# Where the pieces of a side matrix are loaded from: GpSimd's queue or the weights' queue

## The chip, the cores and the metric

One Trainium2 chip; the program runs on one NeuronCore. The metric is the device time of one execution in microseconds. Three executions of the kernel before took 2799.04, 2801.40 and 2794.86 us; the median is 2799.04 us.

## What is computed

Two transformer blocks, one after the other, on 256 tokens of width 2048, in float32. The second block also sees 256 context tokens (`ctx`). Both streams of the second block are normalised and then shifted and scaled by vectors that come out of one big matrix:

```python
def adaln(cond, w_ada, b_ada):
    return jnp.split(jax.nn.silu(cond) @ w_ada + b_ada, ADA_CHUNKS, axis=-1)
...
m_lat = [m[:, None, :] for m in adaln(c, w_ada[l], b_ada[l])]
m_ctx = adaln(c_ctx, w_ada[l], b_ada[l])
hc = modulate(rms_norm_2(ctx, norm1_g[l]), m_ctx[0], m_ctx[1])
h = modulate(rms_norm_2(x, norm1_g[l]), m_lat[0], m_lat[1])
```

`w_ada` is 2048 x 12288 in float32, 100.7 MB, and is multiplied by one vector (two for the first third). It depends on nothing that the first block computes, so the kernel works on it beside the other matrices, long before it is needed.

## The kernel before, in words

**The weights.** All other matrices are cut into 870 pieces of 128 x 1024 (512 KB) in the order of their use. SyncE's queue (SP) loads each into one of four buffers `w` (L204). `Stream.prep` (L231) splits a piece into two float32r halves: ScalarE copies it to `h` (L237), VectorE subtracts to get the rest `l` (L238); there are five buffers of each. A piece is two **slabs** of 128 x 512. TensorE multiplies slab by slab, feature-major (L359, eight matmuls for each slab) or token-major (L392, L393 and L395, six for each slab when there are 256 tokens, twelve in the projection of keys and values). After each slab `Stream.done` (L257) is called: it prepares whatever pieces have a free buffer (`fill`), adds the stage's pace to a credit, and for each whole credit runs one step of the side matrix. In the program, which fixes the order of every engine's queue, the preparation therefore runs about four pieces (eight slabs) ahead of TensorE.

**The side matrix.** `w_ada` is cut into 192 pieces of 128 x 1024, with two buffers `v0` and `v1`. One step is one multiply-and-reduce on VectorE of a piece by a row that is spread over the partitions (L536). Each of the first 64 pieces takes two steps (two conditions), the others one. When the last step of a piece has been written down, `vload` (L207) writes down the load of the piece after next into the buffer that the step has just read, as a DMA on GpSimd's queue (L211). That queue works in order: the load waits for the reduction, and what the program puts on GpSimd after it waits too. `finish` (L225) runs the steps that are left when a stage needs them. `ada_begin` (L513) loads the two rows for the next pieces, sets how far the steps may go, and holds them back for eight ticks.

**The paces** (L36) in steps for each slab: 0.2 feature-major and 0.3 token-major in the first half of block 1, 0.24 and 0.36 in its feed-forward part, 0.55 while keys and values are projected (L1187), 0.3 while the branches are merged, 0.1 and 0.13 in the last feed-forward part.

**The side work.** `Side.tick` (L165) is called once for each slab and advances small generators that add their instructions between the slabs. One of them is `ctx_norm` (L873). It starts while the feed-forward part of block 1 runs, once the first 64 pieces of `w_ada` are done, and normalises the context: for each of two halves of 128 tokens it loads four parts of 128 x 512 and squares them on ScalarE (L883, L477), takes the root on GpSimd (L429), loads the four parts again (L890), scales them on VectorE (L892), transposes them on TensorE (L452) and splits them. These 16 loads are on GpSimd's queue as well, and go to a ring of two buffers, so that a load waits only for the use of the part two before it:

```python
            for c in range(4):
                z = self.rows()
                nc.gpsimd.dma_start(z, cr[:, t, c * 512:(c + 1) * 512])
                self.sumsq(z, ss[:, c:c + 1])
                yield 3
```

**The feed-forward parts** work in six groups of up to eight feature blocks. A group is 64 slabs feature-major (up and gate) and then 32 slabs token-major (down). The eighth token-major slab of a group needs the group's last product, which ScalarE and VectorE make from the last feature-major result (L367, L368, L949 to L951, L979, L337, L338).

Of the kernel before, what the change touches and what calls it, by code (L numbers as in the profile page):

```python
# [155 lines left out]
class Side:  # L156


    def __init__(self, limit=2):
        self.q, self.urgent, self.active, self.now, self.limit, self.per = deque(), deque(), [], 0, limit, 1  # L160
# [30 lines left out]
class Stream:  # L191
# [4 lines left out]
    def __init__(self, nc, w, h, l, v, side):  # L196
        self.nc, self.w, self.h, self.l, self.v, self.side = nc, w, h, l, v, side
        self.items, self.vitems, self.steps = [], [], deque()
        self.loaded = self.mains = self.pos = self.retired = self.vloaded = self.vdone = 0
        self.pace, self.credit, self.limit, self.hold = 0.0, 0.0, 0, 0  # L200

    def load(self):
        while self.loaded < len(self.items) and self.loaded < self.mains + len(self.w):
# [3 lines left out]
    def vload(self):  # L207
        while self.vloaded < len(self.vitems) and self.vloaded < self.vdone + len(self.v):
            src, fns = self.vitems[self.vloaded]
            t = self.v[self.vloaded % len(self.v)]  # L210
            self.nc.gpsimd.dma_start(t, src)  # L211
            self.vloaded += 1
            for k, fn in enumerate(fns):
                self.steps.append((fn, t, k == len(fns) - 1))

    def step(self):
        if not self.steps:
            self.vload()
        fn, t, last = self.steps.popleft()
        fn(t)  # L220
        if last:
            self.vdone += 1
            self.vload()

    def finish(self):  # L225
        while self.vdone < self.limit:
# [30 lines left out]
    def done(self, ahead=True):  # L257

        self.pos += 1
        self.retired = self.pos // 2  # L260
        if not ahead:
            return
        self.fill()
        self.credit += self.pace
        while self.credit >= 1:
            self.credit -= 1
            if self.vdone < self.limit and self.side.now >= self.hold:
                self.step()


class Kernel:
# [200 lines left out]
    def norm_t(self, *args):  # L472
        for step in self.norm_b(*args):
            step()
# [38 lines left out]
    def ada_begin(self, rows, limit):  # L513
        self.ada_rows(rows)
        self.S.limit, self.S.hold = limit, self.side.now + ROWS

    def ada_items(self, names, kind):

        nc, a = self.nc, self.a
        out = []
        two = len(names) > 1
        if two:
            order = [(k, q) for q in range(2) for k in range(32)]
        else:
            order = [(4 * g + k, q) for g in range(4) for q in range(2) for k in range(4)]
        for n, (k, q) in enumerate(order):
            fb = 16 * kind + k
            bias = self.vec("b_ada", fb, 1)  # L530
            fns = []
            for i, name in enumerate(names[k // 16] if two else names):
                col = self.ada_v[name][:, k % 16:k % 16 + 1]

                def fn(w, col=col, slot=i if two else q, begin=col if q else bias):
                    nc.vector.tensor_tensor_reduce(out=self.junk.bitcast(mybir.dt.bfloat16), in0=w,  # L536
                                                   in1=self.adat[:, slot * 1024:(slot + 1) * 1024], scale=1.0,
                                                   scalar=begin, op0=ALU.mult, op1=ALU.add, accum_out=col)
                fns.append(fn)
            if two and n == 31:  # L540
                fns.append(lambda w: self.ada_begin({0: 1, 1: 3}, self.S.limit))
            if n == len(order) - 1:
                fns.append(lambda w: self.ada_end(names, kind))
            out.append((a["wada"][fb, q], fns))
        return out
# [582 lines left out]
    def block2(self):  # L1128
# [324 lines left out]
        for c in range(4):  # L1453
            ba = self.token_major([(oah, oal, 0), (oah, oal, 1)], [self.seg(range(16))],
                                  need=(12, lambda: len(done) == idx and not side.q and not side.active) if c == 0 else None)
            if c == 0:
                side.limit, side.per = 2, 1
                self.pace = PACE[3]
                self.ada_begin({0: 0, 1: 1}, 160)
                gload(0)  # L1460
            g, x = mg["g"][c % 2], mg["x"]
            for t in range(2):
                nc.vector.tensor_mul(g[:, 0, t], ba[t], g[:, 0, t])
            if c < 3:
                gload(c + 1)
            bb = self.token_major([(obh, obl, 0), (obh, obl, 1)], [self.seg(range(8))])
            for t in range(2):
                nc.vector.tensor_mul(g[:, 1, t], bb[t], g[:, 1, t])
                nc.vector.tensor_add(g[:, 0, t], g[:, 0, t], g[:, 1, t])
                side.add(merge_T(g[:, 0, t], c, t))  # L1470
# [122 lines left out]
```

## Time and profile before

| | us |
|---|---|
| median of 3 runs (lowest, highest) | 2799.04 (2794.86, 2801.40) |
| the profiled execution: its own time | 2798.22 |
| the profiled execution: span of the trace | 2796.1 |
| TensorE busy | 2709.5 (97%) |
| VectorE busy | 2017.0 (72%) |
| ScalarE busy | 1335.9 (48%) |
| GpSimd busy | 254.0 (9%) |

How to read it: the span is cut off at the first and last instruction; the execution's own time holds some 2 us more. PE is TensorE's matmuls, DVE VectorE, ACT ScalarE, POOL GpSimd, SP SyncE. "Busy" of PE is an upper bound, since matmuls overlap; whether TensorE is held up is better seen from what ended its idle time, and from the same work timed in two places. A timeline row gives the start and the duration of an instruction and, in square brackets, how long its engine had been idle before it and what ended that.

### The profile page before, as it was taken

The numbers are of one execution on the slowest core, as the hardware profiler recorded it, in microseconds if no ns is written. First come the engines' busy times: TensorE is split into PE (matmuls) and PEld (weight loads), VectorE is DVE, ScalarE is ACT, GpSimd is POOL, SyncE is SP. The second block draws the span as 40 slices with busy tenths as digits, with TensorE's granted clock in tenths as the row PEclk, the third lists the DMA queues.
The fourth block names the chain that finished last, engine by engine and source line by source line (L and its number), as shares of the span: only waits on it lengthen the run. The fifth ranks groups of instructions, "written<-read, shape, count | busy, mean of one in ns | idle before, by whom it ended". The sixth has DMA issues, their size and how long they took to land.

```text
span 2796.1 us, 36791 instructions
## 1 busy us (share of the span) xinstructions
PE 2709.5 (97%) x13654; PEld 2281.2 (82%) x13654; DVE 2017.0 (72%) x2938; ACT 1335.9 (48%) x1994; POOL 254.0 (9%) x397
## 2 busy tenths in 40 slices
PE   8999899999998799999999999999999999999999
PEld 6888787888877688787877788888878888888887
DVE  6888787888877676746567777768766666665566
ACT  5544454545453455522256665544454444444443
POOL 1121000000001100213111010011100000000000
PEclk9999999999998899999999999999999999999999
DMA  7577567676767675565755544489847776766565
GB/s 283 188 235 270 188 211 256 222 257 227 264 223 249 211 234 171 188 231 177 247 188 173 175 163 153 143 302 327 296 162 235 229 234 227 236 205 190 189 201 168
DMA packets 167860, 609.95 MB, mean 218 GB/s; under 512 B 19504, under 2 KB 19696, under 8 KB 166656
## 3 DMA queue, kind: packets, MB, share of 16 engines
q1 hardware_dynamic: 127728, 461.43, 49.1%
q0 software_dynamic: 39808, 145.92, 15.8%
q8 instruction: 107, 1.75, 0.3%
q14 instruction: 73, 0.60, 0.1%
q10 hardware_dynamic: 144, 0.25, 0.0%
HBM read 592.81 MB, written 14.71 MB: 217 GB/s over the span
## 4 chain that ended last, share of the span: by engine, by line
PE 74%; DVE 6%; issue 4%; ACT 3%; DMA 2%; POOL 1%; ACTq 0%; DVEq 0%; POOLq 0%
PE bank L359 29%; PE bank L392 14%; PE bank L393 14%; PE bank L395 14%; DVE l L238 2%; DMA G<-ctx 1%; ACT h L237 1%; DVE G L536 1%; PE bank L342 1%; PE bank L343 1%; PE bank L344 1%; PE bank L1288 1%; PE bank L452 0%; ACT G L477 0%; ACT G L459 0%
## 5 line engine op out<-in xcount | busy, mean ns | idle before, releaser
L238 DVE TENSOR_TENSOR l<-w,h 128x1024 fp32r<-128x1024 f32 x870 | 1063.0, 1228 | 429.8 <-ACT h L237 418.9
L237 ACT CAST h<-w 128x1024 fp32r<-128x1024 f32 x870 | 908.4, 1051 | 591.8 <-PE bank L393 408.7
L359 PE MATMUL bank<-pair,h 128*128 128x512 f32 x3072 | 847.6, 397 | 11.8 <-ACT h L237 11.8
L359 PEld LDWEIGHTS bank<-pair,h 128*128 128x128 f32 x3072 | 529.4, 190 | 82.4 <-ACT h L237 12.6
L392 PE MATMUL bank<-h,pair 128*128 128x512 f32 x1344 | 535.4, 398 | 11.3 <-DVE slot L1203 5.9
L393 PE MATMUL bank<-h,pair 128*128 128x512 f32 x1344 | 526.9, 392 | 1.4 <-DVE pair L338 0.7
L359 PEld LDWEIGHTS bank<-pair,l 128*128 128x128 f32 x3072 | 472.6, 189 | 66.9 <-DVE l L238 0.4
L359 PE MATMUL bank<-pair,l 128*128 128x256 f32 x3072 | 489.9, 281 | 0.0
L395 PE MATMUL bank<-l,pair 128*128 128x512 f32 x1344 | 413.4, 393 | 6.0 <-DVE l L238 5.9
L536 DVE CUSTOM_DVE_ANT_0 G<-v,G 128x1024 bf16<-128x1024 f32 x256 | 329.3, 1286 | 23.6 <-DMA v<-wada 22.6
L392 PE MATMUL bank<-h,slot 128*128 128x512 f32 x768 | 303.2, 395 | 10.6 <-ACT slot L337 7.2
L392 PEld LDWEIGHTS bank<-h,pair 128*128 128x128 f32 x1344 | 253.9, 189 | 69.6 <-issue 12.9
L395 PEld LDWEIGHTS bank<-l,pair 128*128 128x128 f32 x1344 | 254.0, 189 | 63.1 <-DVE l L238 9.0
L393 PE MATMUL bank<-h,slot 128*128 128x512 f32 x768 | 302.5, 394 | 2.0 <-DVE slot L338 2.0
L393 PEld LDWEIGHTS bank<-h,pair 128*128 128x128 f32 x1344 | 253.9, 189 | 52.8 <-DVE pair L338 2.7
L395 PE MATMUL bank<-l,slot 128*128 128x512 f32 x768 | 240.3, 393 | 0.0
L211 POOL DMA_DIRECT2D v<-wada x192 | 102.1, 532 | 1424.2 <-DVE G L536 1371.2
L367 ACT COPY G<-bank 128x256 f32<-128x256 f32 x192 | 71.4, 372 | 263.9 <-PE bank L359 263.9
L392 PEld LDWEIGHTS bank<-h,slot 128*128 128x128 f32 x768 | 146.3, 191 | 42.2 <-ACT slot L337 8.5
L393 PEld LDWEIGHTS bank<-h,slot 128*128 128x128 f32 x768 | 146.3, 191 | 33.9 <-DVE slot L338 3.4
L395 PEld LDWEIGHTS bank<-l,slot 128*128 128x128 f32 x768 | 145.8, 190 | 30.7
L368 DVE TENSOR_TENSOR G<-bank,G 128x256 f32<-128x256 f32 x192 | 81.1, 422 | 121.9 <-ACT G L367 121.7
(217 smaller groups left out, 1710.0 us busy)
## 6 DMA issues: line engine op xcount, KB each, us to landing
v<-wada POOLq DMA_DIRECT2D x192, 512.0 KB, 4.9
w<-wup SPq DMA_DIRECT2D x176, 512.0 KB, 4.4
w<-wgu SPq DMA_DIRECT2D x176, 512.0 KB, 4.0
w<-wdn SPq DMA_DIRECT2D x88, 512.0 KB, 4.5
w<-wfd SPq DMA_DIRECT2D x88, 512.0 KB, 4.0
w<-w SPq DMA_DIRECT2D x66, 512.0 KB, 4.3
w<-w2g SPq DMA_DIRECT2D x64, 512.0 KB, 3.6
w<-w2kv SPq DMA_DIRECT2D x52, 512.0 KB, 4.2
```

The source lines that it names most:

```text
L211: self.nc.gpsimd.dma_start(t, src)
L237: self.nc.scalar.copy(h, w)
L238: self.nc.vector.tensor_sub(l, w, h.bitcast(F32))
L342: t.matmul(out, ah, bh, start=start, stop=False)
L343: t.matmul(out, ah, bl, start=False, stop=False)
L359: t.matmul(bank[:, :size], w[:, j * P:(j + 1) * P], x[:, kb, :size], start=s == n == 0, stop=s == 3 and n == 7)
L367: self.nc.scalar.copy(z, bank[:, 256:])
L368: self.nc.vector.tensor_add(out, bank[:, :256], z)
L392: self.nc.tensor.matmul(banks[i], xh, h, start=seen[i] == 1, stop=False)
L393: self.nc.tensor.matmul(banks[i], xl, h, start=False, stop=False)
L395: self.nc.tensor.matmul(banks[i], xh, l, start=False, stop=seen[i] == total[i])
L536: nc.vector.tensor_tensor_reduce(out=self.junk.bitcast(mybir.dt.bfloat16), in0=w, in1=self.adat[:, slot * 1024:(slot + 1) * 1024], scale=1 ...
```

## The change

The load of a side piece moves from GpSimd's queue to SP's, which loads the weights. It is written down two calls of `done` after the last step of the piece before it in the same buffer (`vdue` counts them), after that call's `fill`. Calls with `ahead` false (the last slabs of a stage) don't count. `step` still loads at once when nothing is left, and `ada_begin` loads the first pieces when there is none yet.

```diff
-        self.pace, self.credit, self.limit, self.hold = 0.0, 0.0, 0, 0
+        self.pace, self.credit, self.limit, self.hold, self.vdue = 0.0, 0.0, 0, 0, 0
...
     def vload(self):
...
-            self.nc.gpsimd.dma_start(t, src)
+            self.nc.sync.dma_start(t, src)
...
     def step(self):
...
         if last:
             self.vdone += 1
-            self.vload()
+            self.vdue = 2
...
     def done(self, ahead=True):
...
         self.fill()
+        self.vdue -= 1
+        if self.vdue == 0:
+            self.vload()
         self.credit += self.pace
...
     def ada_begin(self, rows, limit):
         self.ada_rows(rows)
         self.S.limit, self.S.hold = limit, self.side.now + ROWS
+        if not self.S.steps:
+            self.S.vload()
```

## Rows read from the trace of the kernel before

**Rows 1.** the page's part 1: busy us (share of the span) xinstructions

```profile
PE 2709.5 (97%) x13654; PEld 2281.2 (82%) x13654; DVE 2017.0 (72%) x2938; ACT 1335.9 (48%) x1994; POOL 254.0 (9%) x397
```

**Rows 2.** waits, 820 to 1010 us: engine, line <- releaser: us, times, longest

```profile
POOL v L211 <- DVE G L536: 120.4, 21, 13.3
ACT G L477 <- DMA G<-ctx: 32.3, 5, 7.8
...
PE bank L452 <- DVE G L892: 12.5, 4, 5.0
PE bank L359 <- ACT h L237: 11.8, 3, 5.9
DVE G L892 <- DMA G<-ctx: 11.8, 3, 4.7
...
PE bank L392 <- ACT h L237: 3.3, 1, 3.3
...
PE bank L392 <- ACT slot L337: 2.4, 1, 2.4
...
PE bank L393 <- DVE slot L338: 1.7, 1, 1.7
```

**Rows 3.** timeline of GpSimd: start, us, instruction [idle before, what ended it]

```profile
822.92 0.53 POOL L211 DMA_DIRECT2D v<-wada  x1 [13.31 <-DVE G L536]
823.72 0.54 POOL L883 DMA_DIRECT2D G<-ctx  x1 [0.27 <-ACT G L949]
...
929.48 0.53 POOL L211 DMA_DIRECT2D v<-wada  x1 [10.47 <-DVE G L536]
930.00 0.54 POOL L883 DMA_DIRECT2D G<-ctx  x1
```

**Rows 4.** timeline of ScalarE: the first square of the context

```profile
808.06 0.63 ACT L477 ACTIVATE G<-G 128x512 f32<-128x512 f32 x1 [5.92 <-DMA G<-ctx]
```

**Rows 5.** stretches: us, PE, PEld, DVE, ACT, POOL busy, PEclk, DMA share, GB/s

```profile
687.73:731.30 43.57, 43.57 (x192) 35.80 (x192) 40.84 (x54) 18.68 (x21) 3.17 (x6) 1.00 0.79 264
731.30:820.75 89.45, 89.45 (x513) 78.21 (x512) 72.25 (x112) 48.23 (x78) 5.82 (x11) 1.00 0.71 235
820.75:882.41 61.66, 52.23 (x207) 41.55 (x206) 46.62 (x72) 23.62 (x33) 8.53 (x16) 0.89 0.73 254
882.41:1006.40 123.99, 101.66 (x534) 87.45 (x533) 85.10 (x138) 56.96 (x101) 14.59 (x27) 0.90 0.66 221
1165.00:1400.00 235.00, 229.14 (x994) 188.48 (x994) 138.78 (x209) 55.93 (x65) 49.82 (x72) 0.99 0.64 217
1835.00:2012.00 177.00, 177.00 (x798) 146.46 (x797) 141.22 (x171) 74.25 (x81) 23.42 (x45) 1.00 0.89 317
```

**Rows 6.** timeline of TensorE: one set of context transposes

```profile
858.64 0.60 PE L452 MATMUL bank<-G 128*128 128x128 f32 x4
```

**Rows 7.** the loads of the context at L883

```profile
DMA to landing us min/median/max: 3.2/4.7/8.6
```

**Rows 8.** timeline of VectorE: last product of the group that ends at 731 us

```profile
696.92 0.42 DVE L338 TENSOR_TENSOR slot<-G,slot 128x256 fp32r<-128x256 f32 x1
```

**Rows 9.** SyncE's waits, whole span: engine, line <- releaser: us, times, longest

```profile
SPq L204 <- DVE l L238: 1819.9, 675, 21.3
```

**Rows 10.** the page's part 6, side pieces: KB each, median us to landing

```profile
v<-wada POOLq DMA_DIRECT2D x192, 512.0 KB, 4.9
```

**Rows 11.** loads issued from 1835 to 2012 us: KB each, median us to landing

```profile
v<-wada POOLq DMA_DIRECT2D x32, 512.0 KB, 5.7
...
slot<-gate POOLq DMA_DIRECT2D x8, 512.0 KB, 9.8
```

**Rows 12.** L536's idle before it (us, times), 1165 to 1400 us

```profile
  DMA v<-wada: 15.4, 11
```

**Rows 13.** the page's part 5: VectorE's two largest groups for a slab

```profile
L238 DVE TENSOR_TENSOR l<-w,h 128x1024 fp32r<-128x1024 f32 x870 | 1063.0, 1228 | 429.8 <-ACT h L237 418.9
...
L536 DVE CUSTOM_DVE_ANT_0 G<-v,G 128x1024 bf16<-128x1024 f32 x256 | 329.3, 1286 | 23.6 <-DMA v<-wada 22.6
```

## The prediction

> **What bounds the kernel now.** I read the page first. TensorE is busy 97% of the span [rows 1], so most of the time cannot be touched by moving a load; only the places where TensorE is held up can. I then cut the span into stretches of 20 us and looked for those where TensorE is idle or its granted clock is below 1.00. They are the start, the norms between the parts, two chunk ends while keys and values are projected, and one long one from 820 to 1006 us that has no norm of its own. Its waits [rows 2] say what it is: TensorE waits for VectorE's L892 (12.5 us), for ScalarE's copy L237 (11.8 and 3.3) and for the two halves of a product (2.4 and 1.7), 31.7 us in all. VectorE and ScalarE in turn wait for loads of the context, 11.8 and 32.3 us. In the same stretch GpSimd waits 120.4 us for L536, ahead of loads of side pieces.
>
> GpSimd's timeline joins the two [rows 3]. At 823.72 a context load is issued 0.8 us behind a side load that had waited 13.31 us for its reduction; at 930.00 another stands right behind a side load that had waited 10.47. The context load had nothing of its own to wait for: 0.27 us in one case, none in the other. ScalarE's square then waits, up to 7.8 us [rows 2], and the weight copy that TensorE needs is queued behind the square. The loop feeds itself: a stalled TensorE delays the next side reduction, which delays the next side load, which delays the next context load.
>
> What this costs is read against the same work next door [rows 5]. The token-major part of the group before took 43.57 us, the feature-major part 89.45. With the context work beside them they take 61.66 and 123.99, so 18.1 + 34.5 = 52.6 us more. Some of that is work: 15 and 21 extra matmuls, nine sets of four transposes at up to 0.60 us [rows 6], 5.4 us. About **47 us** are loss: 31.7 idle, the rest the clock, which is granted at 0.89 and 0.90 there against 1.00 before; that is a mean of full rate and the lower level of 1.2 GHz, which follows each idle stretch.
>
> **The change, part by part.**
>
> *Off GpSimd's queue.* All 192 side loads go. What stood behind them in the stretch above are 16 context loads and two roots (L429). A context load then waits only for its ring buffer: the square or split of the part two before it. Squares are three slabs apart, so a load can be out six slabs ahead, 6 x 1.40 = 8.4 us in the feature-major part (1.40 = 89.45/64). Landing takes 4.7 us in the middle, 8.6 at most [rows 7]. When scaling, parts are nine slabs apart and the lead is longer still. So nearly all of the waits should go. GpSimd's own 0.53 us for each issue hid beside other work and counts for nothing; should that cover be missing it would be a gain.
>
> *What stays.* The first context load is asked for and used at once; ScalarE's 5.92 us wait for it [rows 4] remains, bar what a free queue gives. TensorE doesn't stop at that point, being eight slabs ahead, but the lag is carried into the group's end. There is no room there: in the group before, the last product is done at 696.92 + 0.42 = 697.3 [rows 8], and TensorE reaches the slab that needs it at 687.73 + 7 x 1.36 = 697.3 (1.36 = 43.57/32). So of the 7.5 us idle before that slab now (3.3 + 2.4 + 1.7) I keep 3, and 2 for the clock, in the ratio of lost clock to idle above: **5 us**, with bounds of 0 (lag caught up) and 10 (the whole lag and its clock).
>
> *Into SP's queue.* SP waits for nothing new. Between a reduction and the load written down two slabs later lies exactly one prepared piece, and its weight load waits for the L238 that stands behind the reduction on VectorE. SP spends 1819.9 us on that very wait [rows 9]; when it gets to the side load, the reduction is long done. The weight loads behind it are not held by a semaphore, only by the transfer: 512 KB more in the same queue. The bytes are the same as before, and the weights are four pieces ahead. I take 0 for that, 2 at worst.
>
> *Two slabs late.* This is the cost. A buffer is used again two steps later. In the feature-major part at 0.24 that is 8.3 slabs, 11.7 us, against 2.8 for the two slabs plus 4.9 to land [rows 10]: room. In the merge at 0.3 it is 6.67 slabs, 9.07 us, against 2.72 + 5.7 [rows 11] = 8.4: just room. In the one token-major part at 0.36 with one-step pieces it is 5.56 slabs, 7.56 us, against 2.72 + 4.9 = 7.6, and with whole slabs sometimes five, 6.8 us: up to 0.8 us of waiting on VectorE for each of 11 steps, where it was busy 40.84 of 43.57 us without context work [rows 5]. In the projection of keys and values at 0.55 a slab is 2.72 us; two steps are 9.9 us against 5.44 + 4.9. There 44 steps in 80 slabs leave eight pairs on neighbouring slabs; the second of a pair resets the count, both buffers are then reloaded together and the next step waits the full landing, 4.9 us. Eight such waits are 39 us against 15.4 now [rows 12]. VectorE has 235 - 138.8 = 96 us free there and 177 - 141.2 = 36 in the merge [rows 5], so most of it is hidden by the pieces prepared ahead; it shows only where it meets a chunk's end. I take **3 us** on the path for all of this; bounds 0 and 10. The Trainium skill prices a transfer lower, on its page "DMA: Bandwidth & Descriptors", section "Anatomy of one DMA — SWDGE (gpsimd) path", as 2.0 us and the bytes at 436 GB/s: by it a piece would take an estimated 3.2 us, no step but those behind a pair would wait, the 3 us would shrink towards 0 and the sum to 2757; the trace's 4.9 does not agree, and decides.
>
> *Everything else.* Steps are written down at the same slabs as before, so VectorE, ScalarE and TensorE keep their order. `finish` has nothing left to run at its calls, in the trace of before, so its way of loading two at a time stays unused. The first two side pieces are loaded some eight slabs earlier, among the weights, where TensorE is no longer short of them: 0, at worst 1.
>
> The sum against the profiled execution: 2798.2 - 47 + 5 + 3 = 2759.2. That execution is 0.8 us under the median of the runs, so I forecast **2760 us**. The forecast's own bounds are 2799 - 47 = 2752, 2 to 3 lower if the transposes were over-priced, so 2749, and 2799 - 47 + 10 + 10 + 3 = 2775.
>
> **The rivals.**
>
> *Half of it.* The context loads come on time from the queue but land late: if the 8.6 us of the slowest is the rule beside the weights, a square waits for as much as its row now shows less the 10 us or so of queueing, and with the lag at the group's end about half the loss stays: 2799 - 24 = 2775, up to 2781. Against it: the median of 4.7.
>
> *No change.* A DMA is a DMA: the same bytes cross the same engines from either queue, so the landing sets the pace and the queue does not. Then it stays at 2799. The Trainium skill says so on its page "DMA: Bandwidth & Descriptors", section "Issuing engines are not separate DMA queues": transfers from all issuing engines share the same DMA engines and interleave, and a second issuer saves only the usually small time of issuing; by that rule the gain would be next to nothing. Against it stand the 13.31 and 10.47 us which are waits ahead of the issue [rows 3], not transfers.
>
> *Slower: side pieces land after they are needed.* With the load written after one L238, two steps can't be closer than reduction, subtraction and landing, (1.286 + 1.228 + landing)/2 for each [rows 13]. In the merge a step falls every 1.36/0.3 = 4.53 us, so the mechanism decides from a landing of 6.55 us on; the row there says 5.7, and 9.8 for another load of the same size [rows 11], with DMA busy 0.89 of the time. If side pieces in SP's queue took 9.8, a step would take 6.16 us: 32 x 1.63 = 52 us less the lead of 11, so 41. In the projection it would be some 40 x (6.16 - 4.95) = 48 less a lead of 22, so 27. That is 2760 + 68 = 2828. The Trainium skill, same page, section "Queues, rings and completion order", has each DMA engine take turns between its queues, packet by packet; by that a side load in the weights' own queue loses its turns and stands behind whole weight loads, which is the direction of this case. No row here shows the order within a queue. For the case speaks the thin margin of 0.85 us; against it, that weights and side pieces are both asked for at the pace of L238 and the bytes are unchanged.
>
> **How the numbers follow.** The forecast 0.77, half of it 0.11, no change 0.05, slower 0.07. A measurement of this kernel can tell about 0.2%, 5.6 us. The first two cases lie below 2793.4: faster 0.88; same 0.05; slower 0.07. The range takes the forecast's bounds and the half case, 2748 to 2781; the two others, 0.12, stay out.
>
> **What would show it.** Right: no side load on GpSimd; from 820 to 1006 us the two parts close to 45 and 92 us with the clock near 1.00; ScalarE's wait for the context down from 32.3 us to a few, and TensorE's waits at L452 and L359 there gone; a single stall left, at the last product near 830 us. VectorE's idle before L536 up from 22.6 us over the span [rows 13] to some 50, most of it between 1165 and 1400 us, with TensorE's time there within a few us of before. Wrong: context loads issued early and still waited for; TensorE idle from 1835 to 2012 us, where it has none now [rows 5]; or SP's waits for L536 of more than a microsecond or two, with weight copies waiting behind them.

## The result and the profile after

The changed kernel takes 2769.14 us (median of four runs, 2764.35 to 2772.05), the kernel before 2796.95 beside it. The ratio is 0.9897, with a 95% interval of 0.9879 to 0.9916. That is 27.8 us gained, or 1.0%, where 39 were forecast (2799 to 2760). The profiled execution is the slowest of the four, 2772.05 us with a span of 2769.9.

Both kernels issue the same 13,654 matmuls in the same order, so the start of a given matmul in one profile can be taken from its start in the other. The difference, followed from the first matmul to the last, shows where time was gained: 1.9 us ahead of the context, 30.4 us between 820 and 1006 us of before, then 2.3 us lost while keys and values are projected and 3.7 lost in the merge.

The page's part 1 answers to [rows 1]; GpSimd has 192 instructions fewer.

```profile
PE 2697.3 (97%) x13654; PEld 2272.0 (82%) x13654; DVE 2014.7 (73%) x2938; ACT 1335.6 (48%) x1994; POOL 153.0 (6%) x205
```

GpSimd's timeline in the context's stage answers to [rows 3]: start, us, instruction, and in brackets the idle time before and what ended it. Nothing but its ring of two buffers holds a context load now; no side load stands ahead of one.

```profile
826.84 1.11 POOL L895 DMA_DIRECT2D G<-ctx  x2
843.66 0.54 POOL L895 DMA_DIRECT2D G<-ctx  x1 [15.71 <-DVE pair L341]
857.59 0.54 POOL L895 DMA_DIRECT2D G<-ctx  x1 [13.39 <-DVE pair L341]
```

The waits of that stage, 795 to 980 us, answer to [rows 2] (L897 is the scale that was L892, L455 the transposes that were L452, L541 the reduction that was L536, L480 the square that was L477).

```profile
PE bank L455 <- DVE G L897: 10.0, 5, 3.7
DVE G L541 <- DMA v<-wada: 8.9, 7, 2.7
ACT G L480 <- DMA G<-ctx: 7.9, 2, 4.4
...
PE bank L396 <- DVE slot L341: 1.7, 1, 1.7
PE bank L395 <- ACT slot L340: 1.2, 1, 1.2
```

ScalarE's 7.9 us for the context are 4.4 for the first load of all, which was 5.92 [rows 4], and 3.6 in the two parts, where it was 32.3 [rows 2]. VectorE's wait for the context is gone, and so are TensorE's waits for ScalarE's copy. What is left is the stall of 2.9 us at the group's last product, and TensorE's wait for the scale, 10.0 us in five pieces, little less than the 12.5 of before. VectorE's wait for side pieces has grown, from 2.0 us in this stage to 8.9. The two parts of the stage, [rows 5] (us; PE, PEld, DVE, ACT, POOL busy; PEclk; DMA share; GB/s), take 54.2 and 101.1 us where 45 and 92 were forecast and 61.7 and 124.0 stood before:

```profile
819.09:873.25 54.16, 47.47 (x207) 38.43 (x206) 43.65 (x69) 21.85 (x31) 2.71 (x5) 0.97 0.75 271
873.25:974.35 101.10, 94.78 (x534) 81.95 (x533) 86.25 (x140) 59.68 (x105) 7.15 (x13) 0.98 0.79 276
```

VectorE's wait for side pieces over the span rose from 22.6 us [rows 13] to 96.9, twice what was forecast: 8.9 here, 59.8 between 1100 and 1400 us, 26.8 in the merge. The page's parts 5 and 6:

```profile
L541 DVE CUSTOM_DVE_ANT_0 G<-v,G 128x1024 bf16<-128x1024 f32 x256 | 329.3, 1286 | 97.8 <-DMA v<-wada 96.9
...
v<-wada SPq DMA_DIRECT2D x192, 512.0 KB, 5.0
```

A side piece lands as fast from SP's queue as before (5.0 us against 4.9 in [rows 10]). So the pieces are late because they are asked for late. One case, step by step, from SP's and VectorE's timelines:

```profile
845.26 0.42 SPq L211 DMA_DIRECT2D v<-wada  x1
846.01 2.67 SPq L204 DMA_DIRECT2D w<-wdn  x2
848.73 0.42 SPq L211 DMA_DIRECT2D v<-wada  x1
```

```profile
840.62 0.08 DVE L541 DVE_READ_ACCUMULATOR2_ANT G<- 128x1 f32 x1
...
845.90 1.28 DVE L541 CUSTOM_DVE_ANT_0 G<-v,G 128x1024 bf16<-128x1024 f32 x1
847.11 0.08 DVE L541 DVE_READ_ACCUMULATOR2_ANT G<- 128x1 f32 x1
847.11 1.22 DVE L238 TENSOR_TENSOR l<-w,h 128x1024 fp32r<-128x1024 f32 x1
850.00 1.28 DVE L541 CUSTOM_DVE_ANT_0 G<-v,G 128x1024 bf16<-128x1024 f32 x1 [1.68 <-DMA v<-wada]
851.22 0.08 DVE L541 DVE_READ_ACCUMULATOR2_ANT G<- 128x1 f32 x1
851.22 0.48 DVE L897 TENSOR_SCALAR G<-G 128x512 f32<-128x512 f32 x1
```

The reduction is over at 847.2; its buffer is asked for at 848.73, only behind the weight load that waits for the next L238. The piece asked for at 845.26 is one of the later ones: its buffer was free at 840.7, 4.6 us earlier. It lands at 849.9, so VectorE stands for 1.68 us, and the scale L897 stands behind it. TensorE's timeline shows who pays, in its first row:

```profile
851.75 1.12 PE L455 MATMUL bank<-G 128*128 128x128 f32 x4 [3.74 <-DVE G L897]
...
1283.49 0.77 PE L395 MATMUL bank<-h,pair 128*128 128x512 f32 x1 [5.35 <-DVE slot L1208]
...
1902.11 0.66 PE L1452 MATMUL bank<-G,slot 128*128 128x128 f32 x4 [1.95 <-DVE slot L1474]
```

The other two rows are the two later losses, one event each, where TensorE waits for VectorE at the end of a chunk.

### The profile page after: what moved, and what is told of

Its sections match the earlier page's. It is cut to its first block, busy times and chain, and to the rows that moved or that the text cites. A ratio compares the mean times of both kernels' runs of the same rounds, so it can differ in the third digit from the quotient of the medians.

```text
span 2769.9 us, 36650 instructions
## 1 busy us (share of the span) xinstructions
PE 2697.3 (97%) x13654; PEld 2272.0 (82%) x13654; DVE 2014.7 (73%) x2938; ACT 1335.6 (48%) x1994; POOL 153.0 (6%) x205
## 4 chain that ended last, share of the span: by engine, by line
PE 59%; issue 15%; DVE 8%; DMA 3%; ACT 3%; POOL 0%; SPq 0%; DVEq 0%; ACTq 0%; POOLq 0%
PE bank L362 19%; PE bank L395 12%; PE bank L396 12%; PE bank L398 12%; DVE l L238 3%; DMA v<-wada 2%; ACT h L237 1%; DVE G L541 1%; PE bank L345 1%; PE bank L347 1%; PE bank L346 1%; PE bank L1293 1%; DMA G<-ctx 0%; ACT G L480 0%; DVE G L955 0%
## 5 line engine op out<-in xcount | busy, mean ns | idle before, releaser
L238 DVE TENSOR_TENSOR l<-w,h 128x1024 fp32r<-128x1024 f32 x870 | 1061.2, 1226 | 367.1 <-ACT h L237 353.2
L541 DVE CUSTOM_DVE_ANT_0 G<-v,G 128x1024 bf16<-128x1024 f32 x256 | 329.3, 1286 | 97.8 <-DMA v<-wada 96.9
L395 PEld LDWEIGHTS bank<-h,pair 128*128 128x128 f32 x1344 | 254.4, 189 | 72.9 <-issue 16.1
L395 PEld LDWEIGHTS bank<-h,slot 128*128 128x128 f32 x768 | 145.1, 189 | 36.8 <-ACT slot L340 7.3
L398 PEld LDWEIGHTS bank<-l,slot 128*128 128x128 f32 x768 | 145.0, 189 | 30.4
L1310 ACT ACTIVATE G<-bank,G 128x512 f32<-128x512 f32 x64 | 49.8, 780 | 45.0 <-DVE G L1304 44.8
```

Source lines behind the costliest of these rows:

```text
L238: self.nc.vector.tensor_sub(l, w, h.bitcast(F32))
L395: self.nc.tensor.matmul(banks[i], xh, h, start=seen[i] == 1, stop=False)
L398: self.nc.tensor.matmul(banks[i], xh, l, start=False, stop=seen[i] == total[i])
L1310: nc.scalar.activation(d, bank, AF.Exp, bias=mx, scale=rq, accum_out=s)
```

## The experiments

Each was timed beside the kernel before on one chip. The median of before there is 2796.75 us for e1 to e4, 2796.95 for e5 to e8 and 2797.61 for e10 and e11. Us are medians; ratios are to before, with 95% intervals.

| kernel | side loads on | slabs behind | other edit | us | ratio |
|---|---|---|---|---|---|
| changed | SP | 2 | none | 2769.1 | 0.9897 (0.9879 to 0.9916) |
| e1 | GpSimd | 2 | none | 2771.9 | 0.9905 (0.9892 to 0.9919) |
| e2 | SP | 0 | none | 2757.8 | 0.9858 (0.9845 to 0.9872) |
| e3 | SP | 1 | none | 2761.9 | 0.9870 (0.9854 to 0.9885) |
| e4 | GpSimd | 0 | context loads on SP | 2809.2 | 1.0042 (1.0030 to 1.0055) |
| e5 | SP | 2 | own count per buffer | 2767.4 | 0.9888 (0.9874 to 0.9903) |
| e6 | SP | 0 | first context loads early | 2754.1 | 0.9843 (0.9828 to 0.9857) |
| e7 | SP | 0 | transposes later | 2757.5 | 0.9851 (0.9835 to 0.9867) |
| e8 | GpSimd | 4 | own count per buffer | 2767.6 | 0.9891 (0.9877 to 0.9906) |
| e10 | SP | 0 | early, and margin moved | 2753.2 | 0.9845 (0.9831 to 0.9858) |
| e11 | SP | 2 | early, and margin moved | 2765.1 | 0.9886 (0.9873 to 0.9900) |

### e1: the lateness without the queue

```diff
-            self.nc.sync.dma_start(t, src)
+            self.nc.gpsimd.dma_start(t, src)
```

> The side loads go back to GpSimd's queue and stay two slabs late. Theory (the gain is that context loads no longer stand behind a side load that waits for its reduction; lateness is a cost): a context load now stands behind a reduction that is at least two slabs old, so it is issued up to 2.8 us earlier than before the change but not free; the lateness still costs the 6 us seen in the keys/values and merge stages. About 2785 us, 2775 to 2797. Rival A (only the queue counts): nothing gained, the lateness paid, 2797 to 2803. Rival B (the lateness is the gain, by letting reductions finish ahead of the issue): about 2769, as the changed kernel.

2771.9 us: rival B's time, and my theory's is missed by 13 us. Nearly the whole gain is to be had on GpSimd's own queue. Its timeline shows how:

```profile
842.23 0.53 POOL L211 DMA_DIRECT2D v<-wada  x1 [5.16 <-DVE G L541]
842.75 0.54 POOL L895 DMA_DIRECT2D G<-ctx  x1
...
894.36 0.53 POOL L211 DMA_DIRECT2D v<-wada  x1 [10.47 <-DVE G L541]
894.88 1.08 POOL L888 DMA_DIRECT2D G<-ctx  x2
```

A context load still stands behind a waiting side load, but behind that of an older reduction. And the side loads are not asked for late. From the records of each side load between 797 and 985 us I took the time from the end of the last reduction to the issue: its median is 0.30 us over 25 loads, as before the change, against 1.95 in the changed kernel (over the whole span it is under 0.5 us for 178 of 190 loads). GpSimd has nothing else to do, so it reaches the load early and stands there until the reduction is done, two slabs later in the program or not. On that queue the two slabs change the order alone. On SP, which goes in step with VectorE's L238, they are time.

What was true of my theory: context loads stood behind waiting side loads. What was false: that another queue was needed for it. The queue's own part is still seen: the context's stage gains 23.6 us in this profile and 30.4 in the changed kernel's, and ScalarE waits 16.1 us for the context in place of 7.9. The two medians are not told apart, since e1 loses nothing later, where the changed kernel loses 6 us.

### e2 and e3: the queue without the lateness, and with half of it

```diff
-            self.vdue = 2
+            self.vload()        (e2)
+            self.vdue = 1       (e3)
```

> SP's queue as in the changed kernel, but each side load is written down at once behind its reduction, as before the change. Theory: SP already stands at waits for the weights' subtraction, which VectorE does in the same order as the reductions, so the load's wait holds up nothing; VectorE's 97.8 us of idle before the reduction fall to about 25, the 10.0 us in which TensorE waits for the context's scale fall to 3 or less, the 6 us of the keys/values and merge stages come back: 2752 to 2758 us. Rival A (the two slabs protect SP's queue: a waiting side load holds the weight loads behind it): SP waits for the reduction in its list by 100 us or more, ScalarE's copies wait for weights, 2775 or more. Rival B (lateness costs nothing, the rest of the loss is the context loads' own landing): 2767 to 2771.

> SP's queue, one slab late in place of two. Theory: between the changed kernel and the one without lateness, about 2762 us (2756 to 2767), VectorE's idle before the reduction about 60 us. Rival B (lateness costs nothing): 2767 to 2771 as with two.

2757.8 and 2761.9 us, both as the theory has it; with the changed kernel's 2769.1 the three make a series by slabs. The intervals of e2 and the changed kernel lie apart: two slabs cost 11.3 us. That of e3 overlaps both. VectorE's wait for side pieces is 20.4, 34.5 and 96.9 us over the span. In e2 the profile of SP's waits (us, times, longest) shows side loads waiting, which rival A feared:

```profile
SPq L204 <- DVE l L238: 1551.8, 674, 20.8
SPq L211 <- DVE G L541: 224.7, 163, 17.2
```

It does no harm: SP's four largest waits at L204 fell by a little more, from 2153.1 us in the changed kernel (1730.0 + 163.3 + 146.4 + 113.4) to 1911.3 (1551.8 + 149.8 + 127.6 + 82.1). It is the same wait under another name. Reduction and L238 are done by VectorE in the order in which SP waits for them. In the context's stage e2 gains 37.0 us, and TensorE's wait for the scale is 4.3 us instead of 10.0.

### e4: the context loads moved instead

```diff
-                nc.gpsimd.dma_start(z, cr[:, t, c * 512:(c + 1) * 512])
+                nc.sync.dma_start(z, cr[:, t, c * 512:(c + 1) * 512])
```

This is done at both places in the kernel before.

> The kernel before, with its 16 context loads alone moved to SP's queue; the 192 side loads stay on GpSimd's, at once behind their reductions. Theory: the gain is these 16 loads, so nearly all of it is here, and without lateness: 2752 to 2760 us, with GpSimd waiting as long as before for reductions. Rival A (the 192 side loads cost something by themselves on GpSimd's queue, or context loads hold up weights on SP's): 2775 or more. Rival B (the rest of the loss is the context loads' landing): 2765 to 2770.

2809.2 us, slower than before by 0.42% (0.30 to 0.55). My theory is far off, and rival A has the side. Its reasons explain little of it: the side loads wait longer for their reductions than they did (154.4 us from 795 to 1000 us against 120.4), but the context loads no longer stand behind them; and ScalarE's waits for weights in the stage grew only from 8.0 us to 11.2 (5.9 + 2.1 against 6.4 + 4.8). SP's timeline, and ScalarE's at a square:

```profile
812.57 0.33 SPq L204 DMA_DIRECT2D w<-wdn  x1
813.00 0.37 SPq L883 DMA_DIRECT2D G<-ctx  x1
```

```profile
816.83 0.63 ACT L477 ACTIVATE G<-G 128x512 f32<-128x512 f32 x1 [5.05 <-DMA G<-ctx]
```

The second context load has a free buffer, yet is issued 0.1 us behind a weight load, and SP's weight loads are those that wait for L238 [rows 9]; ScalarE stands for 5.05 us. All five context loads from 799 to 850 us stand so, right behind a weight load. ScalarE's wait for the context from 795 to 1000 us is 51.7 us, against 38.2 there before. So SP's queue is as bad a place for these loads as GpSimd's was: both have a wait for VectorE's recent work ahead of them. What counts is not which engine issues, but what waits ahead.

### e5: a count for each buffer

```diff
-            self.vdue = 2
+            self.due.append(self.slabs + 2)
...
-        self.vdue -= 1
-        if self.vdue == 0:
-            self.vload()
+        self.slabs += 1
+        while self.due and self.due[0] <= self.slabs:
+            self.due.popleft()
+            self.vfree += 1
+            self.vload()
```

`vload` then loads up to `vfree` plus the two buffers.

> The changed kernel (SP's queue, two slabs late), but each buffer counts its own two slabs, so that the second piece of a pair on neighbouring slabs no longer puts off the load of the first. Theory (half of VectorE's wait in the keys/values stage is such pairs): its 59.8 us there fall to about 30, the longest from 5.2 to 4 us or less, the 2.3 us lost there come back, the 3.7 us of the merge, which has no pairs, stay: about 2766 us, 2764 to 2768. Rival (the lateness itself, not the pairs): the 59.8 us hardly change, 2768 to 2771.

2767.4 us, which the intervals do not tell from 2769.1: inconclusive on the time. VectorE's wait in the keys/values stage went from 59.8 to 52.7 us, not to 30, so pairs on neighbouring slabs are the smaller part of it. The loss at 1283 us is not in this profile; as e11's profile, with the pairs as in the change, has hardly any of it either (TensorE's longest wait there is 3.6 us against 5.35), the edit can't be credited. The loss in the merge stays, 4.2 us, as expected of a stage without pairs.

### e6: the first context loads early

```diff
+        first = [self.rows() for _ in range(2)]
+        for c, z in enumerate(first):
+            nc.gpsimd.dma_start(z, cr[:, 0, c * 512:(c + 1) * 512])
         while len(self.ada_done) < 8:
             yield 1
...
-                z = self.rows()
-                nc.gpsimd.dma_start(z, cr[:, t, c * 512:(c + 1) * 512])
+                z = first.pop(0) if first else self.rows()
+                if t or c > 1:
+                    nc.gpsimd.dma_start(z, cr[:, t, c * 512:(c + 1) * 512])
```

(on top of e2)

> SP's queue without lateness (2757.8 us), with the first two context loads issued ahead of the wait for the last reduction, many slabs early. Theory (the stall at the group's last product near 830 us comes from ScalarE's 4.5 us wait for the first context load): the wait and the two halves' 1.3 + 1.7 us of TensorE idle go, with the clock's part: about 2753 us, 2751 to 2755. Rival (that stall comes from the stage's crowded VectorE, busy 19.3 of 21 us there): it stays, 2757 to 2759.

2754.1 us against e2's 2757.8, in the expected band; the intervals overlap, but the profile shows the mechanism. ScalarE's wait for the context has left the list, and the stall at the last product with it; TensorE's only wait from 795 to 980 us is this one (the edit adds four lines, so L901 is the scale):

```profile
PE bank L455 <- DVE G L901: 3.4, 2, 2.0
```

The context's stage gains 43.1 us in this profile, 6.1 more than in e2's.

### e7, e10 and e11: more slabs between scale and transposes

```diff
 (e7, on top of e2)
-                yield 4
+                yield 6
                 self.norm_t([z], t, hh, hl, self.gc1, self.ada_v["csh1"], c)
 (e10, on top of e6; e11, on the changed kernel with e6's edit)
-                yield 3
+                yield 1
                 nc.vector.tensor_scalar_mul(z, z, r)
-                yield 4
+                yield 6
```

> SP's queue without lateness (2757.8 us), with each context part's transposes six slabs behind its scale in place of four. Theory (TensorE meets the transposes in order before VectorE has scaled): the 4.3 us of TensorE waiting for the scale and its part of the clock go: about 2752 us, 2750 to 2755. Rival (the lag only moves on, to the splits and the next context part): 2756 to 2760.

2757.5 us: the rival. TensorE's waits for the scale are gone, and its gain up to 987 us of before is 8 us larger than e2's (44.9 against 37.0), but the context's work is now 16 slabs longer and runs into the next group's end, where 6 us are lost; the same two halves of a product are late again:

```profile
973.14 0.50 PE L395 MATMUL bank<-h,slot 128*128 128x512 f32 x1 [1.85 <-ACT slot L340]
974.17 0.50 PE L396 MATMUL bank<-h,slot 128*128 128x512 f32 x1 [0.53 <-DVE slot L341]
```

> SP's queue without lateness, the first two context loads early (2754.1 us), and each context part's scale one slab behind its load in place of three, its transposes six behind the scale in place of four, so that the whole stays as long as it was. Theory (a context load on a free queue needs no slabs ahead of its scale, TensorE needs them between scale and transposes): the 3.4 us of TensorE waiting for the scale and their part of the clock go, nothing moves into the group's end: about 2749 us, 2746 to 2752. Rival (VectorE then waits for the context loads): 2754 or more, with VectorE waiting for the context.

2753.2 us, between the theory's band and the rival's, and not told apart from e6's 2754.1. TensorE's wait for the scale is down to 0.6 us, VectorE waits 1.8 us for the context, and the profile gains 46.2 us up to 987 us of before; 2.2 of them are lost at the group's end, without an idle row. This is the fastest of the kernels by its median, level with e6; both beat the changed kernel.

> The changed kernel, two slabs late as it is, with the same two edits on the context alone. Theory (of what the forecast missed, the context stage's part is the scale being late for the transposes, 10.0 us of TensorE idle and the clock behind it, and the group's end 2.9 us): these go, 14 to 18 us, the 6 us of the keys/values and merge stages stay: about 2753 us, 2750 to 2757. Rival (the late side pieces hold VectorE up wherever the slabs are put): 2760 or more, TensorE idle for the scale by 5 us or more.

2765.1 us: the rival's time again, though not its sign, since TensorE waits only 2.4 us for the scale, not 5 or more. With the side pieces late, the margin buys some 4 us, which the intervals do not tell from none, and not 14 to 18. Against e10, which differs in the lateness alone, it is 11.9 us slower, the 11.3 of e2 and the changed kernel once more. The waits from 795 to 980 us show TensorE's spread over more places, and VectorE's for side pieces as in the changed kernel:

```profile
DVE G L541 <- DMA v<-wada: 10.4, 6, 2.7
...
PE bank L362 <- ACT h L237: 4.5, 4, 1.4
...
PE bank L455 <- DVE G L901: 2.4, 3, 1.4
PE bank L362 <- DVE l L238: 2.0, 2, 1.9
```

The same view of e10 has this for the side pieces:

```profile
DVE G L541 <- DMA v<-wada: 1.2, 2, 1.0
```

The stage, up to 1006 us of before, is 10.2 us longer than e10's, and VectorE waits 9.2 us more in it. Between e2 and the changed kernel it is 7.8 us of VectorE's wait (1.1 against 8.9) and 6.6 of the stage. So in both pairs the stage goes by VectorE, nearly microsecond for microsecond.

### e8: order by four slabs on GpSimd's queue

The edit is e5's with `+ 4`, and the side loads on `nc.gpsimd`.

> Side loads on GpSimd's queue, four slabs behind their reductions in place of two, each buffer with its own count. Theory, after the runs so far (on GpSimd's queue, which runs ahead until a wait stops it, the slabs are a matter of order and not of time: they put context loads ahead of side loads): VectorE's wait for side pieces stays near the 36.8 us of the run with two, context loads get 2.8 us more lead, about 2762 us, 2757 to 2767. Rival (slabs are lateness there too): VectorE waits more than 60 us, 2771 or more.

2767.6 us, half a microsecond outside the theory's band and well short of e2. Two slabs more of order (and a count for each buffer) bring 4 us against e1, which the intervals do not tell from none. VectorE's wait for side pieces is 53.0 us, nearer to e1's 36.8 than to the 96.9 of slabs that are time; but GpSimd still waits 100.5 us for reductions in the stage and ScalarE 16.7 for the context, as in e1. Order on a waiting queue can't do what a free queue does.

## Why the prediction was right, and what it mis-sized

**What bounds it: right.** The stretch from 820 to 1006 us held the loss, and it could be cured nearly in full. I priced it at 47 us; e10 gains 46.2 there and gives 2.2 back.

**Off GpSimd's queue: right in the result, wrong in one reason.** The wait went where I said it would, and the queue alone (e2) gains 38.9 us of the 42 that my sum has without the lateness (47 - 5). But I took the queue to be the only cure and the two slabs to be a price only. e1 shows that on GpSimd's queue the same two slabs, which delay the median load by nothing there, give 24.9 us (2796.75 - 2771.87).

**The first context load and the group's last product, 5 us: the place and the idle part right, the clock's part not.** The stall came at 830 and 832 us, 1.21 and 1.74 us, which is the 3 that I kept. The 2 for the clock were rounded up: my own ratio (15.3 to 31.7) gives 1.4. And the lower level does not follow each idle stretch, as I wrote: in the changed kernel the granted clock is 1.00 from 819 to 840 us, through this stall, and 0.95 from 840 to 873, where TensorE waits 3.74 us; in e2, with the same stall of 1.3 and 1.7 us, it is 0.92 from 819 to 840. e6 removes the stall from e2: 3.7 us by the medians, which the intervals don't tell from none, 6.1 by the profiles.

**SP's queue, 0 us: right.** SP has no wait for the reduction in the changed kernel, and in e2, where it has 224.7 us of them, nothing behind suffers.

**Two slabs late, 3 us: this is the step that failed.** It measured 11.3 us (e2) and 11.9 (e10 against e11), a little over the upper bound of 10 that I gave it. The delay itself was not under-priced: on SP it is 1.5 to 2.0 us in the median of a stage, one L238 and a little, and 2.5 in the mean of all 190 loads, where I had the 2.72 or 2.8 of two slabs. What I got wrong is who covers it. I wrote down up to 0.8 us of waiting for each of 11 steps in the token-major part, 8.8 us, beside a VectorE that was busy 40.84 of 43.57 us, and then let the free time of two other stages hide most of it. The context's stage has no free time. Its busy VectorE was in my own rows: 46.62 us of work in the first part and 85.10 in the second [rows 5], which is 131.7 us in the 137 (45 + 92) to which I expected the stage to shrink. A wait of 8.9 us does not fit there. By profiles the changed kernel loses 6.6 us to it (37.0 - 30.4) in this stage, and 6.0 at the two chunk ends; e11 loses 10.2 against e10 in the stage and under 1 later. Which chunk end meets a late piece changes from one kernel to the next; the total, 11.3 and 11.9 us, hardly does. Whether a third buffer for the side pieces would hide the delay was not tried.

With 11.3 in place of 3 the sum gives a gain of 47 - 5 - 11.3 = 30.7 us; 27.8 were measured. The 2.9 us left are of the size of the transposes' own wait for the scale, 4.3 us in e2, which I had expected to go and which no pair of runs resolves.

**The rivals.** *Half of it*, 2775, is nearer to the measured time than my 2760, but it has not the mechanism: context loads at L888 land in 3.2, 5.8 and 8.2 us (least, median, most), slower than before, and ScalarE still waits for them only 7.9 us. *No change* is out: the page "DMA: Bandwidth & Descriptors" of the Trainium skill, section "Issuing engines are not separate DMA queues", holds as to landing, 4.9 us and 5.0 from either queue, but the time it would give, 2799, is met by none of the kernels that free the context loads, and e4, with the same bytes on another queue, is slower by 12 us. *Slower* needed a landing of 6.55 us in the merge; from 1835 to 2000 us 31 side pieces land in 5.9 us in the median, 0.2 more than before [rows 11]. The sign that I had named against myself, TensorE idle from 1835 to 2012 us, did come, but it is the one stall of 1.95 us above.

## What to carry to other kernels

A load costs what waits ahead of it in its issuer's order: before moving one, list the waits that the new queue stands at, and put loads that need a lead on a queue with none for recent work. Writing a load down later was a free change of order on an idle engine that runs ahead (GpSimd, 0.30 us with and without), and real lateness on one that keeps pace with the consumer (SP, 1.5 to 2.0 us). Before a wait is called hidden, add up the covering engine's work for the stage at its new length, not its old one: the time that the change takes out is the slack that hid it.

## What the runs showed that was not expected

Asking for a piece 2.4 us later in the mean than e2 does became 76.5 us more waiting on VectorE (96.9 against 20.4 in e2) and 11 to 12 us of time. With one slab, where 97 of 190 loads are over 1 us late and the mean is 1.1 us over e2's, it was 14.1 us more waiting (34.5) and 4 us. So twice the delay cost five times the waiting. That room in the schedule is used up first is the likely reason; no run shows it by itself.

TensorE's granted clock was a loss of its own after an idle stretch: between 1270 and 1300 us of the changed kernel it is 0.89 around one wait of 5.35 us, a mean of 2.4 GHz and the lower level of 1.2 GHz, and between 1895 and 1910 us again 0.89 around a wait of 1.95.
